# Expert order computed before the first gather, 18 weight places from the start, overflow branch moved to the 29th expert, last four experts' rows added from SBUF

## The chip, the cores and the metric

One NeuronCore of a Trainium2 chip. The metric is device time in microseconds (us); the slowest core is the only one.

## What is computed

512 tokens of width 1024 go through two blocks in fp32. The first has a Fourier branch, latent attention and a squared-relu MLP; the second a convolution and mLSTM mixer and then the mixture of experts that the change is about. Cut to that part:

```python
grp = argmax(h @ rg_w + rg_b)                 # 4 groups of 8 experts
top_val, top_idx = lax.top_k(expert_logits[grp], 2)
gate = p_grp * softmax(top_val)
for e in range(32):                           # rows routed to e
    y = (silu(xs @ w_gate[e]) * (xs @ w_up[e])) @ w_down[e]   # 1024 -> 512 -> 1024
    out[rows of e] += gate * y
return rmsnorm(x + out, final_norm_g)
```

Each expert has 6 MB of weights, so 192 MB are read, whatever the routing.

## The kernel before

The first 1097 us (both blocks up to the router) hold nothing that the change touches. There the Stream object has already queued the first expert weights.

**Weights.** A piece is 1 MB (128 x 2048 fp32); an expert has two each of gate, up and down, 192 in all, loaded in the order in which PE uses them: gate and up of expert 0, gate and up of expert 1, down of expert 0, gate and up of expert 2, down of expert 1, and so on. `Stream.issue` (L386 is its transfer) issues them all on SP's queue, and each waits until the load six places ahead of it has landed, or two places ahead in the last 24 loads. `Stream.slot` assigns places in a fixed cycle of 18: seven tiles of pool "we", three of pool "w", eight tiles "wm", of which the last two ("wo") are opened only behind the branch described below; until then `fill` (L1889) lets 16 loads go. A place is reused after PE has read its last half.

**Order of the experts.** Places 0 to 2 of the sequence are fixed experts (FIX = 3). The other 29 are taken by the number of rows that they received, so that tile shapes fit: "wide" places with up to 128 rows (L2003 and L2048), "few" with 64 (L1976, L2039), "quad" with 32 (L1990, L2032). The generator `by_count` (L1908) ranks the experts in four pieces that `gate_up(0)` runs between its own matmuls; its tile `order` is written by L1928, SP reads a register from it for each expert (L398 in `nth`) and uses it as an address. `slots` (L1760, matmuls L1765) and `slot_cols` (L1781) compute row numbers and gate weights for every place.

**Rows.** POOL gathers an expert's rows from DRAM (`gather`, L1816), PE transposes them (`xpose`, L1843), `gate_up` and `hidden_T` (L2019) compute silu(g) * u turned round, `down` the product, and POOL scatters the result to `y` in DRAM (L2053).

**Branch.** After `gate_up(0)` all engines read `last` and take tc.If (L2066) if some expert got more rows than its place holds; its body handles the surplus with small loads on SP (L2082). With these inputs the body is skipped. In program order it stands between the slot matmuls and `xpose(1)` on PE, and among the first dynamic loads on SP.

**End.** For four blocks of 128 tokens, X (the residual x3d) and two halves of y are loaded (`final_loads`, L2157 and L2159) before the last four experts (LASTS = 4) are done, added, normalised and stored (`final_rows`, L2174). The rows of the last four experts then come separately: after their scatters POOL gathers those rows again (L2149), DVE adds and scales them (L2215 to L2221), and POOL scatters them over the output (L2222); the program's close is L2242.

Of the kernel before, what the change touches and what calls it, by code (L numbers as in the profile page):

```python
# [256 lines left out]
def mixer_kernel(ctx: ExitStack, tc: tile.TileContext, io, out, stop=None, dbg=None):  # L257
# [80 lines left out]
    class Stream:  # L338
# [3 lines left out]
        def __init__(self):  # L342
# [4 lines left out]
            self.keep = []  # L347
# [13 lines left out]
        def slot(self, i):  # L361
            j = i - self.first
            if i < 10 and i not in self.ub.values():
                return self.start.tile([128, 2048], F32, tag="w0", name="w0", bufs=7)
            r = j % 18
            if j < 0 or 6 < r < 10:
                return ws.tile([128, 2048], F32, tag="w", name="w", bufs=self.WB)
            return self.keep[r if r < 7 else r - 3]

        def issue(self, upto, queue=nc.sync):  # L370
# [3 lines left out]
            while self.issued[x] <= min(upto, (self.first, len(self.items))[x] - 1):  # L374
# [12 lines left out]
                if x:  # L387
                    n = 6 if len(self.items) - i > 24 else 2
# [1222 lines left out]
    st.keep += [WE.tile([128, 2048], F32, name=f"we{i}") for i in range(7)]  # L1611
# [72 lines left out]
    st.keep += [LE.tile([128, 2048], F32, name=f"wm{i}") for i in range(6)]  # L1684
# [104 lines left out]
    queue_slots(0, A0, pos8)  # L1789
    idxf, idyf = slots("f", RE, [A0], codef, FIX)  # L1790
    later = {}
# [89 lines left out]
    closed("rq")  # L1881
    eunits = [(n, e, h, j) for e, ns in eorder for h in range(2) for j in range(2) for n in ns]
# [4 lines left out]
    passed = [0]  # L1887

    def fill():  # L1889
# [18 lines left out]
    def by_count():  # L1908

        k4 = scratch[0:32, 288:416].rearrange("p (a b) -> p a b", a=4)  # L1910
        kc = scratch[0:32, 488:490]
        rk = scratch[:, 416:424]
        ohr = scratch[:, 0:256].rearrange("p (a b) -> p a b", a=8)
        id32 = ident[0:32, 0:32]
        dve.tensor_tensor(k4[:, 0], key[0:32], id32, op=OP.mult)
        dve.tensor_reduce(kc[:, 0:1], k4[:, 0], AX.X, OP.add)
        dve.tensor_scalar(k4[:, 1], key[0:32], kc[:, 0:1], None, op0=OP.is_gt)
        dve.tensor_reduce(kc[:, 1:2], k4[:, 1], AX.X, OP.add)
        dve.tensor_scalar(k4[:, 2], id32, kc[:, 1:2], None, op0=OP.mult)
        dve.tensor_scalar(k4[:, 3], cst[0:32, 3, 0:32], kc[:, 1:2], None, op0=OP.is_equal)  # L1920
        yield 1
        prk = pmm(128, 64)
        pe.matmul(prk[:, 0:32], ones[0:32], k4[:, 2], start=True, stop=True)
        pe.matmul(prk[0:1, 32:64], pcol[0:32], k4[:, 3], start=True, stop=True)
        order = RE.tile([1, 32], I32, name="order")
        dve.tensor_copy(order, prk[0:1, 32:64])
        st.order = order
        dve.tensor_tensor(ohr, oh8, prk[:, None, 0:32].to_broadcast([128, 8, 32]), op=OP.mult)  # L1928
# [95 lines left out]
    def down(i):  # L2024
        e = seq[i]
        y, h = yt(i), hT[i]
# [28 lines left out]
        if i >= NE - LASTS:  # L2055
            wait_for(scattered[-1], none)

# [7 lines left out]
    rv = nc.values_load(last, min_val=0, max_val=S)  # L2065
    with tc.If(rv > 0):  # L2066
        OV = opened("ov", side="right")
        more = []
        fill_place(code, oh8, 32)
        fill_parts(code, oh8, 32)  # L2070
# [175 lines left out]
```

## Time and profile before

| | |
|---|---|
| runs | 1676.5, 1670.79, 1667.84 us; median 1670.79 |
| profiled execution | 1677.21 us; span 1675.3 us; mean granted TensorE clock 0.954 |
| PE busy | 1507.1 us (90%) |
| DVE, ACT, POOL busy | 713.3 us (43%), 515.2 us (31%), 143.0 us (9%) |
| traffic | 337.77 MB, mean 202 GB/s |
| chain that ended last | DMA 18%, PE 11% of the span |

The times in all rows count from the start of the span. The share of PE is an average: the first 1097 us are one stage, the experts from there to the end another, and the rows below belong to the second.

### The profile page before, as it was taken

How to read it: one execution, taken by the hardware profiler on the slowest of the kernel's cores; microseconds unless marked ns; L12 is line 12 of the kernel's file. 1: busy time of each engine (PE TensorE's matmuls, PEld its weight loads, DVE VectorE, ACT ScalarE, POOL GpSimd, SP SyncE). 2: the span in 40 equal slices, each digit the busy share in tenths (PEclk: the TensorE clock that was granted, in tenths of full speed). 3: DMA queues.
4: the chain of work that ended last, by engine and by line, in shares of the span. 5: the costliest groups of instructions: out<-in, count | busy, mean ns of one | idle time of the engine just before them, and what ended most of it. 6: DMA issues, size and time to landing. Idle time of an engine off the chain costs nothing. (4 is left out here: it accounts for less than half of the span.)

```text
span 1675.3 us, 20140 instructions
## 1 busy us (share of the span) xinstructions
PE 1507.1 (90%) x7857; PEld 1015.2 (61%) x7857; DVE 713.3 (43%) x1251; ACT 515.2 (31%) x852; POOL 143.0 (9%) x162
## 2 busy tenths in 40 slices
PE   5999999999999999999899999958999999977642
PEld 3887577788878888888657767724444444322210
DVE  5757665635663443435637967541111110100023
ACT  3454654534341323224314474300111110111101
POOL 1102310000000000000000000231110111100001
PEclk9999999999999999999999999978999999989865
DMA  9321831032222222222243223558999999999893
GB/s 369 116 84 63 322 147 51 32 121 100 84 101 101 101 77 99 101 90 87 77 117 115 97 101 116 189 186 329 378 418 419 417 403 393 404 404 413 332 371 139
DMA packets 65447, 337.77 MB, mean 202 GB/s; under 512 B 10884, under 2 KB 20268, under 8 KB 28356
## 3 DMA queue, kind: packets, MB, share of 16 engines
q1 hardware_dynamic: 54656, 318.27, 49.4%
q0 software_dynamic: 7328, 11.60, 2.1%
q10 hardware_dynamic: 3364, 6.58, 1.4%
q8 instruction: 63, 1.03, 0.2%
q14 instruction: 36, 0.29, 0.1%
HBM read 328.28 MB, written 16.78 MB: 206 GB/s over the span
## 5 line engine op out<-in xcount | busy, mean ns | idle before, releaser
L418 ACT CAST wh<-w 128x1024 fp32r<-128x1024 f32 (+1 forms) x140 | 145.5, 1041 | 366.1 <-PE mm L495 306.2
L420 DVE TENSOR_TENSOR wl<-w,wh 128x1024 fp32r<-128x1024 f32 x136 | 165.8, 1220 | 164.5 <-ACT wh L418 156.7
L496 PE MATMUL mm<-h2H,wl 128*128 128x512 f32 x256 | 101.4, 397 | 0.5 <-DVE wl L420 0.5
L495 PE MATMUL mm<-h2L,wh 128*128 128x512 f32 x256 | 101.6, 397 | 0.0
L494 PE MATMUL mm<-uH,wh 128*128 128x512 f32 x256 | 101.5, 396 | 0.0
L496 PE MATMUL mm<-uH,wl 128*128 128x512 f32 x256 | 101.3, 397 | 0.0
L495 PE MATMUL mm<-uL,wh 128*128 128x512 f32 x256 | 101.3, 396 | 0.0
L494 PE MATMUL mm<-h2H,wh 128*128 128x512 f32 x256 | 100.4, 398 | 0.0
L2003 PE MATMUL mm<-we,xgT 128*128 128x512 f32 x160 | 74.2, 612 | 0.0
L2003 PE MATMUL mm<-wm,xgT 128*128 128x512 f32 x160 | 70.2, 593 | 0.0
L1273 DVE SCALAR_TENSOR_TENSOR xT<-mm,mod,xT 128x512 f32<-128x512 f32 x32 | 24.0, 751 | 99.9 <-PE mm L496 99.9
L495 PE MATMUL mm<-hL,wh 128*128 128x512 f32 x152 | 61.5, 405 | 2.7 <-DVE hL L499 2.7
L494 PE MATMUL mm<-hH,wh 128*128 128x512 f32 x152 | 62.8, 413 | 0.3 <-ACT hH L772 0.3
L496 PE MATMUL mm<-hH,wl 128*128 128x512 f32 x152 | 61.3, 403 | 0.0
L496 PEld LDWEIGHTS mm<-h2H,wl 128*128 128x128 f32 x256 | 48.2, 188 | 12.6 <-DVE wl L420 1.0
L494 PEld LDWEIGHTS mm<-h2H,wh 128*128 128x128 f32 x256 | 48.2, 188 | 11.9 <-ACT wh L418 0.4
L495 PEld LDWEIGHTS mm<-uL,wh 128*128 128x128 f32 x256 | 48.2, 188 | 11.8
L494 PEld LDWEIGHTS mm<-uH,wh 128*128 128x128 f32 x256 | 48.2, 188 | 11.8
L496 PEld LDWEIGHTS mm<-uH,wl 128*128 128x128 f32 x256 | 48.2, 188 | 11.7
L495 PEld LDWEIGHTS mm<-h2L,wh 128*128 128x128 f32 x256 | 48.2, 188 | 11.6
L2003 PEld LDWEIGHTS mm<-we,xgT 128*128 128x128 f32 x160 | 30.8, 197 | 36.2 <-issue 36.0
L2003 PEld LDWEIGHTS mm<-wm,xgT 128*128 128x128 f32 x160 | 30.0, 190 | 36.0 <-issue 35.4
(626 smaller groups left out, 3079.3 us busy)
## 6 DMA issues: line engine op xcount, KB each, us to landing
w<-in_wd_dram SPq DMA_DIRECT2D x72, 1024.0 KB, 4.8
we<-in_eg_dram SPq DMA_DIRECT2D x34, 1024.0 KB, 15.4
wm<-in_eg_dram SPq DMA_DIRECT2D x30, 1024.0 KB, 15.7
wm<-in_eu_dram SPq DMA_DIRECT2D x30, 1024.0 KB, 15.0
we<-in_eu_dram SPq DMA_DIRECT2D x23, 1024.0 KB, 15.2
w<-in_ed_dram SPq DMA_DIRECT2D x22, 1024.0 KB, 16.2
wm<-in_ed_dram SPq DMA_DIRECT2D x22, 1024.0 KB, 15.4
we<-in_ed_dram SPq DMA_DIRECT2D x20, 1024.0 KB, 15.3
```

What stands on the lines that cost most here:

```text
L418: act.copy(h[:, :n], w)
L420: eng.tensor_tensor(l[:, :n], w, h[:, :n].bitcast(F32), op=OP.subtract)
L494: pe.matmul(o, lh, rh, start=start, stop=False)
L495: pe.matmul(o, lh, rl, start=False, stop=False)
L496: pe.matmul(o, ll, rh, start=False, stop=stop)
L1273: dve.scalar_tensor_tensor(xT[:, m], p, mod[:, 0, 40 + m:41 + m], xT[:, m], op0=OP.mult, op1=OP.add)
L2003: pe.matmul(p, x[k], w[:, z * 512:z * 512 + 512], start=k == 0, stop=k == KC - 1)
```

## The change

1. The ranking that gives `order` (and `places`, a copy for the later steps) is moved from `by_count` to a place ahead of `slots("f", ...)`, before the first gather.
2. The two last places ("wo") are opened before `gate_up(0)`. Places come from a free list instead of a fixed cycle; `fill` issues while a place is free, less `kept[0]` of them.
3. A load waits for the load three ahead of it in the first 18 and in the last 24 loads, and six ahead elsewhere.
4. The branch becomes `beyond_rows`, called at the 29th place (i = N0 = 28); its body loads on ACT's queue instead of SP's.
5. The quad buffer `yq` has two copies instead of three. For the last four places POOL clears the row tile before gathering.
6. The last four experts' rows are copied from PSUM into one SBUF tile `yl`, 32 rows each, not scattered. `final_loads` loads all four blocks at i = 29. At the end PE loads X of three blocks into PSUM by products with `ident`, adds `yl` by products with one-hot matrices `pick`, and all four blocks are squared, scaled and stored there. The last four scatters, POOL's gathers of those rows and the scatter over the output are gone.

```diff
-            r = j % 18
-            if j < 0 or 6 < r < 10:
+            if j < 0:
                 return ws.tile([128, 2048], F32, tag="w", name="w", bufs=self.WB)
-            return self.keep[r if r < 7 else r - 3]
+            self.place[j] = self.free.pop(0)
+            return self.take(self.place[j])
+
+        def take(self, p):
+            return ws.tile([128, 2048], F32, tag="w", name="w", bufs=self.WB) if p == "w" else p
...
-                    n = 6 if len(self.items) - i > 24 else 2
+                    n = 6 if i - self.first > 17 and len(self.items) - i > 24 else 3
...
+    places = scratch[:, 492:524]
+    k4 = scratch[0:32, 288:416].rearrange("p (a b) -> p a b", a=4)
+    kc = scratch[0:32, 488:490]
+    id32 = ident[0:32, 0:32]
+    dve.tensor_tensor(k4[:, 0], key[0:32], id32, op=OP.mult)
+    dve.tensor_reduce(kc[:, 0:1], k4[:, 0], AX.X, OP.add)
+    dve.tensor_scalar(k4[:, 1], key[0:32], kc[:, 0:1], None, op0=OP.is_gt)
+    dve.tensor_reduce(kc[:, 1:2], k4[:, 1], AX.X, OP.add)
+    dve.tensor_scalar(k4[:, 2], id32, kc[:, 1:2], None, op0=OP.mult)
+    dve.tensor_scalar(k4[:, 3], cst[0:32, 3, 0:32], kc[:, 1:2], None, op0=OP.is_equal)
     idxf, idyf = slots("f", RE, [A0], codef, FIX)
+    prk = pmm(128, 64)
+    pe.matmul(prk[0:1, 32:64], pcol[0:32], k4[:, 3], start=True, stop=True)
+    pe.matmul(prk[:, 0:32], ones[0:32], k4[:, 2], start=True, stop=True)
+    order = RE.tile([1, 32], I32, name="order")
+    dve.tensor_copy(order, prk[0:1, 32:64])
+    act.copy(places, prk[:, 0:32])
...
-            ys[i] = LE.tile([128, 256], F32, name="yq", tag="yq", bufs=3) if quad(seq[i]) else h3[2 + wide.index(i) % 2]
+            ys[i] = LE.tile([128, 256], F32, name="yq", tag="yq", bufs=2) if quad(seq[i]) else h3[2 + wide.index(i) % 2]
...
+    WO = opened("wo", side="right")
+    st.free += [WO.tile([128, 2048], F32, name=f"wm{i}") for i in range(6, 8)]
+    
+    st.order = order
...
+            st.free.append(st.place[passed[0]])
             passed[0] += 1
-        q = st.issued[1] - st.first
-        while q < len(last_of) and (q < 16 or len(st.keep) == 15 and q < 18 + passed[0]):
-            st.issue(st.first + q)
-            if st.issued[1] - st.first == q:
-                return
-            q += 1
+        while st.issued[1] < len(st.items) and len(st.free) > kept[0]:
+            st.issue(st.issued[1])
...
+            if i >= NE - LASTS:
+                n = 32 * (i - NE + LASTS)
+                for q in range(4):
+                    (dve.tensor_copy if q % 2 else act.copy)(yl[n:n + 32, q * 256:q * 256 + 256], p[32 * q:32 * q + 32, 0:256])
+                return
...
+    def beyond_rows():
+        rv = nc.values_load(last, min_val=0, max_val=S)
+        with tc.If(rv > 0):
...
+                    act.dma_start(t, src[bass.ds(e, 1)].rearrange("o p n -> (o p) n")[:, j * 512:j * 512 + 512])
+                    return t
...
+    def final_loads():
+        for i in range(4):
+            X.append(st.take(st.free.pop(0)))
+            Y.append(st.take(st.free.pop(0)))
             r = slice(i * 128, i * 128 + 128)
             nc.sync.dma_start(X[i][:, 0:D], x3d[r])
             for z, o in enumerate((X[i][:, D:], Y[i][:, 0:D])):
                 ld = nc.sync.dma_start(o, y2[z * S + i * 128:z * S + i * 128 + 128])
-                for f in scattered[:N0] + [none]:
+                for f in scattered + [none]:
...
+        if i == N0:
+            beyond_rows()
+            yl = h3[0]
+            pick = h3[1][:, 0:512].rearrange("p (i t) -> p i t", i=4)
+            for n in range(4):
+                dve.tensor_scalar(pick[:, n], cst[:, 3], lt[:, 0:1], -128.0 * n, op0=OP.subtract, op1=OP.is_equal)
...
+            if gathered >= N0:
+                pool.memset(xg(gathered), 0.0)
...
+        if i == N0 - 2:
+            kept[0] = 8
+        if i == N0 + 1:
+            assert len(st.free) >= 8
+            kept[0] = 0
+            final_loads()
+        if i > N0 + 1:
+            sums_of_rows(2 * (i - N0 - 2))
         if i == NE - 1:
-            final_rows(0)
+            P = [pbig() for _ in range(2)]
+            P = [[p[:, n] for n in halves] for p in P] + [[pmm() for _ in halves]]
+            for m in range(3):
+                for z, n in enumerate(halves):
+                    pe.matmul(P[m][z], ident, X[m][:, n], start=True, stop=False)
     down(NE - 1)
...
+    P.append([pmm() for _ in halves])
+    for m in range(4):
+        for z, n in enumerate(halves):
+            pe.matmul(P[m][z], pick[:, m], yl[:, n], start=m == 3, stop=True)
+    x3 = X[3][:, 0:D]
+    for z, n in enumerate(halves):
+        dve.tensor_tensor(x3[:, n], x3[:, n], P[3][z], op=OP.add)
+    ss = WO.tile([128, 4, 2], F32, name="ss")
+    for m in range(4):
+        o = Y[m][:, D:]
+        for z, n in enumerate(halves):
+            act.activation(o[:, n], P[m][z] if m < 3 else x3[:, n], AF.Square, accum_out=ss[:, m, z:z + 1])
+        if m % 2:
+            a = slice(m - 1, m + 1)
+            dve.tensor_tensor(fs[:, a], ss[:, a, 0], ss[:, a, 1], op=OP.add)
+            dve.tensor_scalar(v[:, a], fs[:, a], 1.0 / D, EPS, op0=OP.mult, op1=OP.add)
+            r = rsqrt(WO, v[:, a], 2)
+            for k in range(m - 1, m + 1):
+                o = Y[k][:, D:]
+                for z, n in enumerate(halves):
+                    dve.scalar_tensor_tensor(o[:, n], P[k][z] if k < 3 else x3[:, n], r[:, k - m + 1:k - m + 2], fB[:, n],
+                                             op0=OP.mult, op1=OP.mult)
+                nc.sync.dma_start(out[0, k * 128:k * 128 + 128, :], o)
```

**SP behind the 16th load.** L386 (L390 in the changed kernel) is `Stream.issue`, L398 (L402) the register read. Before:

```order
L386 DMA wm_8395<-in_ed_dram 128x2048
L398 TENSOR_LOAD order
L398 ISA x2
...
L386 DMA we_8092<-in_ed_dram 128x2048
L398 TENSOR_LOAD order
L398 ISA x2
L386 DMA we_8093<-in_ed_dram 128x2048
...
L2066 COMPARE_AND_BRANCH
```

Now:

```order
L390 DMA wm_8395<-in_ed_dram 128x2048
...
L402 TENSOR_LOAD order
L402 ISA x2
L390 ISA
L390 DMA wm_8544<-in_eg_dram 128x2048
...
L390 DMA wm_8545<-in_eu_dram 128x2048
...
L390 DMA we_8090<-in_eg_dram 128x2048
L390 ISA
L390 DMA we_8091<-in_eu_dram 128x2048
L2077 TENSOR_LOAD last
L2077 ISA x2
L390 DMA we_8092<-in_ed_dram 128x2048
```

Loads into the two later places follow the first register reads, and the branch no longer stands among the first dynamic loads.

**PE at the end of expert 0.** L1843 (L1864) is the transpose of the next expert's rows, L2019 (L2026) `hidden_T`, L2003 (L2010) the gate and up matmuls. Before:

```order
L1781 MATMUL mm<-code,A_8532 128x6x14
L2065 TENSOR_LOAD last
L2066 COMPARE_AND_BRANCH
...
L2066 UNCONDITIONAL_BRANCH
L1843 MATMUL big<-cst,h_8108 128x128 x8
L2019 MATMUL mm<-cst,es 128x128 x4
L1843 MATMUL big<-cst,h_8107 128x128 x8
L2003 MATMUL mm<-we_8094,xgT 128x512
```

Now:

```order
L1956 MATMUL mm<-cst,pm 1x128
L2010 MATMUL mm<-we_8092,xgT 128x512
L2010 MATMUL mm<-we_8093,xgT 128x512
...
L1864 MATMUL big<-cst,h_8108 128x128 x4
L1785 LDWEIGHTS A
L1785 MATMUL mm<-code,A 128x6x18
...
L1864 MATMUL big<-cst,h_8107 128x128 x8
L2026 MATMUL mm<-cst,es 128x128 x4
L2010 MATMUL mm<-we_8094,xgT 128x512
```

The slot matmuls stand earlier, and PE goes from the transposes to the second expert with no branch between.

**SP at the end.** L2157, L2159 (L2163, L2165) are the loads of X and y, L2174 (L2245) the output stores. Before:

```order
L2159 DMA we_8091<-y 128x1024
L386 ISA
L386 DMA w<-in_ed_dram 128x2048
...
L386 DMA wm_8390<-in_ed_dram 128x2048
L386 ISA
L386 DMA wm_8391<-in_ed_dram 128x2048
L2174 DMA out_dram<-wm_9255 128x1024
L2174 DMA out_dram<-we_8091 128x1024
```

Now:

```order
L390 DMA we_8090<-in_eg_dram 128x2048
L2078 COMPARE_AND_BRANCH
...
L2078 UNCONDITIONAL_BRANCH
L390 ISA
L390 DMA we_8091<-in_eu_dram 128x2048
...
L390 DMA wm_8395<-in_eu_dram 128x2048
L2165 DMA we_8096<-y 128x1024
...
L390 DMA wm_8544<-in_ed_dram 128x2048
...
L2245 DMA out_dram<-w 128x1024 x2
L2245 DMA out_dram<-wm_8391 128x1024
```

The branch stands eleven weight loads before the last; all loads of y come ahead of the last four weight loads; all four stores come at the very end.

## Rows read from the trace of the kernel before

**Rows 1.** Busy time by window: us, PE, PEld, DVE, ACT, POOL (count), PEclk, DMA share, GB/s.

```profile
1112.00:1130.00 18.00, 17.28 (x50) 8.68 (x51) 4.37 (x13) 1.28 (x1) 5.44 (x9) 0.83 0.01 1
...
1170.00:1187.00 17.00, 17.00 (x45) 7.70 (x43) 0.75 (x1) 1.23 (x3) 1.04 (x1) 1.00 0.79 293
1187.00:1330.00 143.00, 143.00 (x861) 68.99 (x859) 16.86 (x32) 19.05 (x33) 20.32 (x20) 0.99 1.01 416
```

**Rows 2.** Waits of SP's queue, 1097 to 1145: total us, times, longest us.

```profile
SPq L398 <- DVE rstd L1928: 27.6, 1, 27.6
SPq L2066 <- SPq L2066: 5.8, 1, 5.8
```

**Rows 3.** Timeline of SP, 1097 to 1146: start us, us, what.

```profile
1130.29 1.33 SPq L386 DMA_DIRECT2D we<-in_ed_dram  x2
1140.87 0.35 SPq L386 DMA_DIRECT2D wm<-in_eg_dram  x1
```

**Rows 4.** Timeline of PE around the branch, with the wait in brackets.

```profile
1131.46 0.84 PE L1781 MATMUL mm<-code,A 128*128 128x108 bf16 x16
1139.69 1.94 PE L1843 MATMUL big<-cst,h 128*128 128x128 f32 x8 [7.38 <-PEq L2066]
...
1143.98 2.23 PE L2003 MATMUL mm<-we,xgT 128*128 128x512 f32 x3
```

**Rows 5.** Chain that ended last, 1290 to 1360.

```profile
1302.17 6.87 PE mm L2003 x16
...
1330.31 16.24 DMA wm<-in_eu_dram
```

**Rows 6.** Busy time by window, second part of the experts.

```profile
1330.00:1548.00 218.00, 193.88 (x1013) 80.08 (x1011) 22.89 (x40) 27.48 (x48) 27.60 (x28) 0.98 1.01 405
1548.00:1558.50 10.50, 8.61 (x40) 2.85 (x40) 1.17 (x2) 2.80 (x5) 0.90 (x1) 1.00 0.57 210
1558.50:1583.50 25.00, 15.89 (x128) 5.96 (x132) 1.19 (x3) 3.16 (x6) 1.79 (x2) 0.77 0.96 361
1583.50:1600.00 16.50, 9.60 (x88) 3.97 (x80) 0.77 (x2) 1.58 (x4) 1.00 (x1) 0.72 1.00 384
...
1558.50:1650.50 92.00, 47.97 (x393) 18.32 (x393) 20.82 (x39) 11.55 (x24) 5.20 (x5) 0.70 0.95 363
```

**Rows 7.** Timeline of SP at the last 24 loads.

```profile
1543.31 0.33 SPq L386 DMA_DIRECT2D we<-in_eu_dram  x1
1556.09 0.33 SPq L386 DMA_DIRECT2D we<-in_eg_dram  x1
```

**Rows 8.** Timeline of all engines after the last weights.

```profile
1650.50 1.93 PE L2032 MATMUL mm<-wm,hT 128*32 128x256 f32 x16 [0.47 <-DMA wm<-in_ed_dram]
...
1652.50 0.37 ACT L2033 COPY yq<-mm 128x256 f32<-128x256 f32 x1 [7.65 <-PE mm L2032]
...
1664.78 0.16 DVE L515 SCALAR_TENSOR_TENSOR nwt<-nwt 128x1 f32<-128x1 f32 x1
...
1666.54 1.02 POOL L2222 DMA_INDIRECT out_dram<-h,li  x1 [8.16 <-DVE h L2221]
```

**Rows 9.** Timelines of ACT, DVE and PE elsewhere.

```profile
1130.29 0.69 ACT L2004 ACTIVATE es<-mm,scf 128x512 f32<-128x512 f32 x1 [13.46 <-PE mm L2003]
...
1131.58 0.75 DVE L2005 SCALAR_TENSOR_TENSOR es<-mm,scf,es 128x512 f32<-128x512 f32 x1 [4.58 <-PE mm L1765]
...
1506.06 1.07 PE L2032 MATMUL mm<-we,hT 128*32 128x256 f32 x16
```

**Rows 10.** DMA issues: count, KB each, us to landing.

```profile
h3d<-h SPq DMA_DIRECT2D x8, 256.0 KB, 2.6
...
out_dram<-wm SPq DMA_DIRECT2D x3, 512.0 KB, 6.8
...
out_dram<-h,li POOLq DMA_INDIRECT x1, 2.6
```

**Rows 11.** Waits of SP's queue after 1650.

```profile
SPq L2242 <- PEq L2242: 5.3, 2, 4.8
```

More of the change, by code (lines that the diff above doesn't have):

```diff
@@ L346, in __init__ @@
             self.issued = [0, 0]
-            self.keep = []
+            self.free = []
+            self.place = {}
             self.taken = 0
@@ L1610, in mixer_kernel @@
     WE = opened("we", side="right")
-    st.keep += [WE.tile([128, 2048], F32, name=f"we{i}") for i in range(7)]
+    st.free += [WE.tile([128, 2048], F32, name=f"we{i}") for i in range(7)] + 3 * ["w"]
     st.issue(st.first + 6)
@@ L1683, in mixer_kernel @@
     LE = opened("le")
-    st.keep += [LE.tile([128, 2048], F32, name=f"wm{i}") for i in range(6)]
+    st.free += [LE.tile([128, 2048], F32, name=f"wm{i}") for i in range(6)]
     with tc.issue_after(x3w[-1].ins):
@@ L1908, in by_count @@
     def by_count():
-        k4 = scratch[0:32, 288:416].rearrange("p (a b) -> p a b", a=4)
-        kc = scratch[0:32, 488:490]
         rk = scratch[:, 416:424]
         ohr = scratch[:, 0:256].rearrange("p (a b) -> p a b", a=8)
[L1914 to L1928, printed above, removed]
+        dve.tensor_tensor(ohr, oh8, places[:, None].to_broadcast([128, 8, 32]), op=OP.mult)
         dve.tensor_reduce(rk, ohr, AX.X, OP.add)
@@ L2025, in down @@
         e = seq[i]
-        y, h = yt(i), hT[i]
+        h = hT[i]
+        if i < NE - LASTS:
+            y = yt(i)
         if quad(e):
@@ L2123, in mixer_kernel, with last_rows @@
     fB = RE.tile([128, D], F32, name="fB")
     N0 = NE - LASTS
-    stores = []
+    assert quad(seq[N0]) and not quad(seq[N0 - 1]) and yt(N0 - 1) is h3[3]
     fs = WO.tile([128, 4], F32, name="fs")
     v = WO.tile([128, 4], F32, name="fv")
+    lt = WO.tile([128, 4], F32, name="lt")
     X, Y = [], []
-    def last_idx():
-        f = RE.tile([128, 4], F32, name="lf")
-        ids = RE.tile([128, 3], I32, name="li")
+    def last_rows():
+        ids = WO.tile([128, 1], I32, name="li")
         for n in range(LASTS):
@@ L2136, in last_idx @@
             e = seq[N0 + n]
[L2137 to L2155 removed]
+            dve.tensor_copy(lt[r, 1:2], later["y"][r, e:e + 1])
+        dve.tensor_tensor(lt[:, 1:2], lt[:, 1:2], cst[:, 4, 112:113], op=OP.subtract)
+        dve.tensor_scalar(lt[:, 1:2], lt[:, 1:2], 0.25, None, op0=OP.mult)
+        dve.tensor_scalar(lt[:, 2:3], lt[:, 1:2], S - 0.5, -float(S), op0=OP.is_ge, op1=OP.mult)
+        dve.tensor_tensor(lt[:, 0:1], lt[:, 1:2], lt[:, 2:3], op=OP.add)
+        dve.tensor_copy(ids, lt[:, 1:2])
+        return ids
+    def final_loads():
+        for i in range(4):
+            X.append(st.take(st.free.pop(0)))
+            Y.append(st.take(st.free.pop(0)))
             r = slice(i * 128, i * 128 + 128)
@@ L2196, in mixer_kernel @@
             p = pbig()
-            for z in range(2):
-                pe.matmul(p[:, z * 512:z * 512 + 512], ident[0:2, z:z + 1].to_broadcast([2, 128]), frow, start=True, stop=True)
+            for z, n in enumerate(halves):
+                pe.matmul(p[:, n], ident[0:2, z:z + 1].to_broadcast([2, 128]), frow, start=True, stop=True)
             act.copy(fB, p)
-        if i >= NE - 3 and i < NE - 1:
-            a = 2 * (i - NE + 3)
-            assert last_of[len(last_of) - 18 + 2 * a + 3] < nu[0]
-            final_loads(a)
@@ L2219, in mixer_kernel @@
-    dve.tensor_scalar(gs[:, 1:2], gs[:, 0:1], 1.0 / D, EPS, op0=OP.mult, op1=OP.add)
-    r = rsqrt(WO, gs[:, 1:2], 1)
-    dve.scalar_tensor_tensor(lz, lx, r, fB, op0=OP.mult, op1=OP.mult)
-    sc = pool.indirect_dma_start(out=out[0], out_offset=bass.IndirectOffsetOnAxis(ap=ids[:, 0:1], axis=0), in_=lz, in_offset=None,
-                                 bounds_check=S - 1, oob_is_err=False)
-    for f in stores:
-        wait_for(sc, f)
+        if i == N0 - 2:
[4 more added lines that the diff above has]
+            final_loads()
@@ new lines, in mixer_kernel @@
+    x3 = X[3][:, 0:D]
[13 more added lines that the diff above has]
+                o = Y[k][:, D:]
+                for z, n in enumerate(halves):
+                    dve.scalar_tensor_tensor(o[:, n], P[k][z] if k < 3 else x3[:, n], r[:, k - m + 1:k - m + 2], fB[:, n],
+                                             op0=OP.mult, op1=OP.mult)
+                nc.sync.dma_start(out[0, k * 128:k * 128 + 128, :], o)
```

148 lines of the change are left out of this document (56 added, 92 removed).

## The prediction

> **What bounds the kernel now.** I read the counts of busy time by window first, then the waits of SP's queue, the timelines around the two places where traffic stops, the chain of waits, and last the tail. The two kernels issue the same work until the router is done, so everything below lies behind 1097 us of the span.
>
> The expert stage moves 192 weight pieces of 1 MB through SP's queue into 16, later 18, places in SBUF. [rows 1] shows its phases, and the DMA column matters most. From 1112 to 1130 almost nothing moves (1 GB/s): all 16 places are full, and SP waits for the order of the experts, 27.6 us of it [rows 2]. The loads restart at 1130.29, are cut again by the branch, and go on at 1140.87 [rows 3]. PE has its own hole: its last matmul before the branch starts at 1131.46, the next at 1139.69 after 7.38 us behind the branch, and the second expert's gate and up begin at 1143.98 [rows 4]. Then, the decisive row: from 1170 to 1187 the DMA share is 0.79 at 293 GB/s while PE is busy for 17.00 of 17 us. The loads had filled every place and waited for PE to free them. So by 1187 the 18 us of silence had been made up, and what the loads could fetch was set by the moment at which PE freed places. From 1187 to 1330 both are full (PE 143.00 of 143 us, 416 GB/s); the stock of full places is eaten, and at 1330.31 the chain changes from PE's matmuls to loads [rows 5]. From there to the end the loads are the bound.
>
> [rows 6] has this second part: 405 GB/s until 1548 with six loads in flight, a hole of 210 GB/s where the rule changes from six to two, then 363 GB/s on average over the last 92 us. PE is busy for 47.97 us of those 92. After the last weights, the tail from 1650.50 to the end of the span at 1675.3 takes 24.8 us and is a serial chain [rows 8].
>
> **The change part by part.** All sums are made against the profiled execution, 1677.2 us; it stands 6.4 us above the median of the runs shown (1670.79), and I subtract the same difference from the median.
>
> *A. Start.* The branch leaves the place after expert 0's gate and up, the slot matmuls move between the halves of that gate and up, and the transposes follow directly. The hole of 7.38 us goes; what remains is the handover. Second expert's matmuls: 1143.98 before, about 1137 now. I take **-7.2** (between -4, if half of the hole returns as a wait for the slots or for expert 0's silu, and -8.5, if the handover before L1843 vanishes too). As PE's frees set the loads' stock at 1187, and the loads set the end, the whole later stage moves with this. The earlier order and the two early places cost and gain nothing more: 29 register reads (32 experts less the three fixed ones) at about 0.57 us (27.6 us of waiting end near 1124.5, ten reads later the first load is issued at 1130.29 [rows 2, 3]) lie in the 18 us of silence; if the order came no earlier than before, the loads would start at 1130 as now, and the slack of the 0.79 row, 17 x 0.21 = 3.6 us, covers half of the shift only. Three in flight for the first 18 loads cost nothing: these land before 1112 and the first of the dynamic ones are not needed until after 1137.
>
> *B. The switch.* In before SP issues nothing between 1543.31 and 1556.09 [rows 7], and the window of 10.5 us runs at 210 instead of 405 GB/s: 10.5 x (1 - 210/405) = 5.1 us lost. Going from six to three instead of two leaves two loads, not one, in flight at the emptiest point. I take half, **-2.5** (0 to -5.1).
>
> *C. The last 24 loads.* Before: 92 us at 363 GB/s are 33.4 MB. The four output stores (2.1 MB) leave this stretch for the tail: 31.3 MB. With two weight loads in flight the row is 361 GB/s; where two weights and half-MB loads overlapped, about three in flight, it is 384; with six it is 405 [rows 6]. The first 17 loads, 17.8 MB, at 384 take 46.4 us; the other 13.5 MB, where half-MB loads come on top, at 405 take 33.3 us; 79.7 together. The branch now stands on SP between load 180 and 181, and its untaken side waits until all of SP's transfers have landed. That empties the pipe of three loads once. Nearest row: the switch's 5.1 us [rows 6]; nothing below, and above the time of three whole loads, 3 x 1.05 MB / 384 = 8.2 us. I take 4.5. Together 84.2 instead of 92: **-7.8** (from 92 to 31.3/0.405 = 77.3 us, -14.7; to 31.3/0.361 + 8.2 = 94.9 us, +2.9). PE and ACT also meet the branch here; the hole of 7.38 us is covered by PE's 44 idle us in this stretch. The y loads that SP issues between load 187 and the last four wait for expert 27's scatter; its weights are loads 170 and 171, at 1.05/0.384 = 2.7 us each some 40 us earlier: nothing. If that cover were gone, the four loads behind on SP would slip with it. Two yq buffers for three and POOL's memsets of gathered rows: nothing, since POOL is busy for 5.20 of the 92 us.
>
> *D. The tail.* Before: 24.8 us from the last down product at 1650.50. Now the rows stay in SBUF: no scatter, no gathers, no scattered store, but the adding is done by PE and all four blocks are finished at the end. Last down product 1.9 [rows 8]; four copies that ACT and DVE make in turn, 0.37 each plus handover, 1.9; eight one-hot products, which are 16 PE instructions of 512 columns: 6.87 at full clock [rows 5]. PE's granted clock in the last 92 us is 0.70 and it has idled just before, as in 1650.50, where 16 instructions took 1.93 against 1.07 at full clock [rows 8, 9]; at 0.65, 10.6. Behind the last product two additions on DVE and the last two squares on ACT, 0.75 x 2 + 0.69 x 2 [rows 9] = 2.9. Then DVE: 16 small operations at 0.2 (the series that ends at 1664.78 is eight steps of 0.19 [rows 8]) and eight scalings at 0.75, 9.2, because in its order the first pair's scaling stands behind the second pair's sum. Store: 0.33 to issue, and between 2.6 us (256 KB) and 6.8 us (512 KB under load) to land [rows 10], I take 3.9. The end: before, the last scatter is issued at 1666.54, lands 2.6 us later, and of the 6.2 us to the end 4.8 are SP's wait for the other engines' close [rows 8, 11], behind POOL's transfer; without it 1.4. The sum is 1.9 + 1.9 + 10.6 + 2.9 + 9.2 + 4.2 + 1.4 = 32.1, **+7.3** (from -2.5, with full clock, a 2.6 us landing and the first pair's work hidden; to +13.9, at half clock, 13.7 us, and 6.8 us to land).
>
> Sum: -7.2 - 2.5 - 7.8 + 7.3 = **-10.2**: 1667.0 for a run like the profiled one, **1661** for the median.
>
> **Rivals.** *R1: the third load in flight gives nothing.* If two in flight already take what the queues give, the last stretch keeps 363 GB/s: 31.3/0.363 + 4.5 = 90.7, C is -1.3, B is 0, and the sum -1.2: **1670**. For it: the row of two in flight shows a share of 0.96 [rows 6], nearly full. Against it: the GB/s beside that share are 361, not 405, so full shares are not full traffic. The Trainium skill, "DMA: Bandwidth & Descriptors", section "Anatomy of one DMA — SWDGE (gpsimd) path", gives a transfer a fixed part of about 2.0 us and its bytes at 436 GB/s; by that fit 1 MB takes 4.4 us and two in flight would offer 477 GB/s, so that an estimate from the page finds two sufficient, and with it R1. The trace disagrees: 361 measured with two.
>
> *R2: slower, the branch in the full stage.* Where the branch stood, queues were nearly idle; now each engine jumps while 384 GB/s run. If SP's jump waits behind the queued loads and the pipe then refills from nothing, one round of three loads costs 8.2 us; three rounds, 24.6 instead of my 4.5, give **1681**. It decides from some 23 us of standstill on. For it: SP waited 5.8 us [rows 2] and PE 7.38 us [rows 4] there even with little traffic. Against it: those holes are well below 23 us, and SP's untaken side holds no loads of the body any more, so its jump is short. The Trainium skill, "Runtime: NRT & Kernel Launch", section "Instruction fetch mechanics", says that a taken branch whose target lies outside the pages already fetched costs a DMA fetch of the target page. PE's 7.38 us agree.
>
> *R3: the silence is regained in full.* If bytes alone bound the end, 18 us of standstill count instead of 7.2: -18 - 2.5 - 7.8 + 7.3 = -21, **1650**. Against it: the 0.79 row, where loads wait for places.
>
> *R4: the start does not move.* If PE at the second expert waits for the slots or the transposed rows until about 1144, A is 0 and the sum -3.0: **1668**. For it: in before silu and slots end only at about 1132 [rows 9].
>
> **Numbers.** About 0.5%, 8.4 us, is what a measurement of this kernel can tell from no change: faster means below 1662.4. My forecast has 0.54 (own range 1654 to 1667): 0.40 below that line, 0.14 within. R1 0.22: 0.03 faster, 0.16 same, 0.03 slower, if its tail is at the long end. R2 0.08, slower. R3 0.12, faster. R4 0.04, same. Together faster 0.55, same 0.34, slower 0.11. The range 1645 to 1673 takes in R3, R1 and R4 and the bounds of the tail, and leaves out R2 and the far ends of A, C and D.
>
> **What would show it.** A: PE's first matmul of the second expert at about 1137 and no wait on a branch there. B and C: over 375 GB/s in the stretch from the switch to the branch, a hole of some 5 us on SP once, and the last weights landing about 17 us earlier than 1650.50 (1633). D: a tail of 32 us after them, with PE's one-hot products 9 to 12 us and no POOL transfer. I am wrong if the loads stay near 361 GB/s (R1), if the hole at the branch is over 20 us (R2), if the last weights land before 1625 (R3), or if the tail is over 39 us.

## The result, and the profile after

The changed kernel takes **1649.8 us** (median of 4 runs, 1646.2 to 1653.2) against 1672.2 us: ratio 0.9866, 95% interval 0.9831 to 0.9901. The forecast was 1661 with a range of 1645 to 1673; the direction holds, the gain is twice what I gave. It lies below the forecast's own range (1654 to 1667); the wide range holds it because that also took in the 1650 of rival R3 and the lower bound of the tail.

The profiled execution takes 1646.16 us (span 1644.3), 31.0 us less than the profiled one of before. Not all of that is the change: the first gate-and-up matmul of expert 0, behind a thousand microseconds of the same work, starts at 1114.71 in the one and at 1109.96 in the other. In the runs of this case it starts anywhere from 1109.96 to 1118.52. So I measure from that matmul, and give totals by medians. Timeline of PE, before (the first line is expert 0's own transposes):

```profile
1112.72 1.94 PE L1843 MATMUL mm<-cst,h 128*128 128x128 f32 x8 [10.48 <-DMA h<-h3d,idxf]
...
1114.71 8.86 PE L2003 MATMUL mm<-we,xgT 128*128 128x512 f32 x16
```

and after:

```profile
1107.97 1.94 PE L1864 MATMUL mm<-cst,h 128*128 128x128 f32 x8 [8.48 <-DMA h<-h3d,idxf]
...
1109.96 8.13 PE L2010 MATMUL mm<-we,xgT 128*128 128x512 f32 x16
...
1118.44 7.03 PE L2010 MATMUL mm<-we,xgT 128*128 128x512 f32 x16
1125.31 0.60 PE L1864 MATMUL big<-cst,h 128*128 128x128 f32 x4
1125.74 0.84 PE L1785 MATMUL mm<-code,A 128*128 128x108 bf16 x16
1126.42 1.50 PE L1864 MATMUL big<-cst,h 128*128 128x128 f32 x12
1127.76 0.60 PE L2026 MATMUL mm<-cst,es 128*128 128x128 f32 x4
```

These answer to [rows 4]: no wait on a branch, and the second expert's matmuls begin at 1128.20. From expert 0 to the next it is 18.24 us, where it was 29.27.

The windows after (us, PE, PEld, DVE, ACT, POOL with counts, PEclk, DMA share, GB/s) answer to [rows 1, 6]:

```profile
1112.00:1130.00 18.00, 18.00 (x89) 9.69 (x88) 5.76 (x24) 2.98 (x3) 6.05 (x6) 1.00 0.57 207
1130.00:1145.00 15.00, 15.00 (x37) 6.63 (x36) 0.75 (x1) 0.69 (x1) 0.00 (x0) 1.00 0.82 305
1145.00:1170.00 25.00, 25.00 (x64) 11.34 (x63) 2.04 (x3) 1.65 (x3) 2.05 (x2) 1.00 0.85 314
1170.00:1187.00 17.00, 17.00 (x173) 8.98 (x175) 3.14 (x7) 2.92 (x7) 3.35 (x4) 1.00 1.00 388
...
1526.00:1537.00 11.00, 9.15 (x38) 2.94 (x38) 0.48 (x2) 1.35 (x3) 0.00 (x0) 1.00 0.80 333
1537.00:1568.60 31.60, 11.55 (x95) 4.42 (x94) 1.09 (x2) 4.61 (x9) 2.69 (x3) 0.80 0.99 385
1568.60:1576.00 7.40, 1.35 (x14) 0.77 (x18) 1.55 (x6) 0.00 (x0) 0.00 (x0) 0.50 0.76 316
1576.00:1622.40 46.40, 31.90 (x322) 13.98 (x314) 14.72 (x21) 5.07 (x13) 0.00 (x0) 0.81 0.95 385
...
1537.00:1622.40 85.40, 44.80 (x423) 19.17 (x422) 17.37 (x29) 9.68 (x22) 2.69 (x3) 0.78 0.95 379
...
1622.40:1631.60 9.20, 8.21 (x32) 3.38 (x32) 1.54 (x3) 4.09 (x13) 0.00 (x0) 1.00 0.01 2
```

Four things stand there. PE has no idle time from 1112 to 1187, at granted clock 1.00 where the first of these windows had 0.83 [rows 1]. The queues are still not full until 1170, now because the loads wait for places; the wait table of SP from 1110 to 1300 names the main releaser (31.2 of its 31.5 us lie before 1170):

```profile
SPq L390 <- PE mm L2010: 31.5, 10, 8.4
```

From the switch on it is 385 GB/s with three in flight on both sides of the branch, 379 with the branch in it. The drain at the branch is 7.4 us at 316 GB/s, between two loads 7.65 us apart; SP's waits in 1560 to 1600 (total, times, longest):

```profile
SPq L2078 <- SPq L2078: 6.6, 4, 2.5
```

The tail, from the chain of waits that ended last (start, us, what), answers to [rows 8]:

```profile
1622.46 1.11 PE mm L2041 x16
...
1624.46 1.98 PE big L2226 x4
1626.45 1.73 PE mm L2226 x4
...
1629.65 2.31 ACT w L2234 x8
1631.96 0.58 ACT wm L2234 x2
...
1634.52 2.64 DVE w L2243 x4
...
1639.06 1.32 DVE wm L2243 x2
```

It lasts from 1622.46 to 1644.3, 21.8 us, against 24.8. The split of the change, by distances in the two traces: start -11.0 (18.24 for 29.27), from there to the first of the last 24 loads -3.3 (408.8 for 412.1), from that load to the last down product -8.9 (85.5 for 94.4), tail -3.0. Together -26.2; the medians say -22.4. There is one trace of the kernel before, from its slowest execution (1677.21 us; the others took 1667.84 to 1676.5), so some us of the parts can be chance.

### The profile page after: what moved, and what is told of

The parts are those of the page before. It is cut to its first block, busy times and chain, and to the rows that moved or that the text cites. A ratio compares the mean times of both kernels' runs of the same rounds, so it can differ in the third digit from the quotient of the medians.

```text
span 1644.3 us, 20192 instructions
## 1 busy us (share of the span) xinstructions
PE 1497.1 (91%) x7885; PEld 1011.1 (61%) x7885; DVE 713.6 (43%) x1258; ACT 516.6 (31%) x863; POOL 135.4 (8%) x158
## 3 DMA queue, kind: packets, MB, share of 16 engines
q8 instruction: 65, 1.06, 0.3%
## 5 line engine op out<-in xcount | busy, mean ns | idle before, releaser
L2010 PE MATMUL mm<-we,xgT 128*128 128x512 f32 x160 | 72.5, 601 | 0.0
L2010 PE MATMUL mm<-wm,xgT 128*128 128x512 f32 x160 | 71.9, 605 | 0.0
L2010 PEld LDWEIGHTS mm<-wm,xgT 128*128 128x128 f32 x160 | 30.5, 194 | 36.6 <-issue 36.0
L2010 PEld LDWEIGHTS mm<-we,xgT 128*128 128x128 f32 x160 | 30.3, 193 | 35.6 <-issue 34.8
## 6 DMA issues: line engine op xcount, KB each, us to landing
wm<-in_eg_dram SPq DMA_DIRECT2D x31, 1024.0 KB, 15.4
wm<-in_eu_dram SPq DMA_DIRECT2D x31, 1024.0 KB, 15.2
wm<-in_ed_dram SPq DMA_DIRECT2D x22, 1024.0 KB, 15.2
we<-in_ed_dram SPq DMA_DIRECT2D x22, 1024.0 KB, 15.2
```

The costliest lines, as they stand in the source:

```text
L2010: pe.matmul(p, x[k], w[:, z * 512:z * 512 + 512], start=k == 0, stop=k == KC - 1)
```

## The experiments

All medians, ratios (to the kernel before, in the same session) and distances. D1 runs from expert 0's first gate-and-up matmul to the next expert's, D2 to the last down product, D3 to the end of the span. The kernel before had medians of 1670.7 to 1673.8 us beside these runs, so across sessions the ratios compare better than the us.

| kernel | us | ratio, 95% interval | D1 | D2 | D3 |
|---|---|---|---|---|---|
| before | 1672.2 | | 29.3 | 535.8 | 560.6 |
| changed | 1649.8 | 0.9866 (0.9831 to 0.9901) | 18.2 | 512.5 | 534.3 |
| e1 two in flight | 1659.3 | 0.9919 (0.9900 to 0.9938) | 19.1 | 522.5 | 547.2 |
| e2 no branch | 1646.6 | 0.9844 (0.9825 to 0.9863) | 18.6 | 510.3 | 532.1 |
| e3 branch early | 1658.8 | 0.9910 (0.9888 to 0.9932) | 26.3 | 522.3 | 544.2 |
| e4 order late | 1649.8 | 0.9866 (0.9844 to 0.9888) | 18.0 | 513.2 | 535.0 |
| e5 no ident products | 1652.7 | 0.9868 (0.9846 to 0.9890) | 19.1 | 514.8 | 537.1 |
| e6 old ending, no branch | 1654.2 | 0.9881 (0.9866 to 0.9896) | 18.8 | 513.7 | 538.3 |
| e7 four in flight | 1648.8 | 0.9857 (0.9837 to 0.9876) | 18.5 | 513.4 | 535.2 |
| e8 six in flight | 1651.0 | 0.9857 (0.9837 to 0.9877) | 18.2 | 513.5 | 535.3 |
| e9 two places late | 1652.8 | 0.9883 (0.9863 to 0.9904) | 16.8 | | 533.8 |
| e10 six, three at the branch | 1650.2 | 0.9867 (0.9844 to 0.9889) | 18.9 | 514.3 | 536.2 |
| e11 six, no branch | 1649.1 | 0.9864 (0.9844 to 0.9884) | 18.2 | | 532.2 |
| e12 six, body's loads on POOL | 1649.5 | 0.9864 (0.9838 to 0.9891) | 18.9 | 509.6 | 531.5 |

(In e4 and e9 PE does half of the next expert's transposes before expert 0's first gate-and-up matmul, so their distances start about 1.7 us later; counted from expert 0's own transposes, D3 is 536.3 in the changed kernel, 538.8 in e4 and 537.6 in e9. In e9 and e11 the last down products run in one group, and D2 isn't comparable. D1 is 18.2 to 19.1 in the ten traces whose start is that of the changed kernel, so a few tenths of a us in it say nothing.)

**e1, two loads in flight in the last 24.**

```diff
-  n = 6 if i - self.first > 17 and len(self.items) - i > 24 else 3
+  n = 2 if len(self.items) - i <= 24 else 6 if i - self.first > 17 else 3
```

> The changed kernel with two loads in flight instead of three in the last 24 loads. Theory (the third load was worth about 9 us: in the trace the stretch from the first of these loads to the last weights took 94.4 us before and 85.5 after): that stretch comes back to 92 to 95 us, and the time is 1657 to 1660 us. Rival (two loads already take what the queues give, and the gain came from the stores leaving the stretch): the stretch stays at 85 to 87 us and the time within 2 us of 1650.

9.5 us slower than the changed kernel. Its windows around the switch and behind it, then the second one in three parts, before, in and behind the drain at the branch:

```profile
1530.00:1543.40 13.40, 10.93 (x50) 3.75 (x50) 1.42 (x3) 2.42 (x4) 0.90 (x1) 1.00 0.71 295
1543.40:1634.20 90.80, 51.97 (x414) 20.19 (x410) 16.57 (x27) 8.58 (x20) 1.80 (x2) 0.76 0.91 352
...
1543.40:1564.90 21.50, 11.31 (x86) 4.07 (x82) 0.00 (x0) 3.53 (x7) 1.80 (x2) 0.84 0.94 328
1564.90:1571.80 6.90, 2.78 (x26) 1.47 (x30) 1.55 (x6) 0.00 (x0) 0.00 (x0) 0.59 0.64 256
1571.80:1634.20 62.40, 37.89 (x306) 14.65 (x298) 15.02 (x21) 5.05 (x13) 0.00 (x0) 0.74 0.94 370
```

Over the whole stretch 352 GB/s where three give 379, and 328 against 385 between switch and branch. The stretch takes 90.9 us, less than the 92 expected, 5.4 more than with three; the way from the second expert to the first of the last 24 loads grows by 3.8 us (412.6 for 408.8), the tail by 2.8. The third load is worth its time: R1 falls. With two in flight the branch also comes five weight loads earlier, and the loads of y stand ahead of the last ten weight loads instead of the last four; what that adds is not separated.

By the Trainium skill, "DMA: Bandwidth & Descriptors", section "Anatomy of one DMA — SWDGE (gpsimd) path", the estimate worked out from its fit for two transfers of 1 MB in flight was 477 GB/s. That fit is for transfers issued by GpSimd. Here SP issues them, and this run shows 328 to 370 outside the drain.

**e2, no branch; e3, the branch behind expert 0 again.** Of the changed kernel, e2 drops the call, and e3 moves it ahead of the loop over the experts:

```diff
         if i == N0:
-            beyond_rows()
```
```diff
     gathered = 2
+    beyond_rows()
```

> The changed kernel without the overflow branch (its body is skipped with these inputs). Theory (the emptied pipe at the 29th place costs a few us once): the hole between two loads on SP of 7.65 us goes, the last weights land 3 to 5 us earlier, 1645 to 1647 us. Rival 1 (the drain is made up by later loads): 1650. Rival 2 (the branch in the full stage costs more than its hole shows, since PE stood still for 19.6 us): 1640 or less.

> The changed kernel with the branch back behind expert 0's gate and up, all else as changed. Theory (PE's hole at the start sets the whole stage, because the loads wait for places that PE frees): from the first gate-and-up matmul of expert 0 to that of the next expert 25 to 28 us instead of 18.2, the drain near the end goes, and the time is 1649.8 + 8 - 4 = 1653 to 1657 us. Rival (bytes alone bound the end, the first loads are out already, and the PE hole is hidden): 1645 to 1647 us, as without the branch.

By medians the branch costs 3.2 us at the 29th place (1649.8 - 1646.6; the runs overlap, and by D2 and D3 it is 2.2) and 12.2 at the first (1658.8 - 1646.6; the runs lie apart, and by D2 and D3 it is 12.0). Timeline of PE in e3:

```profile
1131.68 0.84 PE L1785 MATMUL mm<-code,A 128*128 128x108 bf16 x16
1138.01 1.08 PE L1864 MATMUL big<-cst,h 128*128 128x128 f32 x4 [5.49 <-PEq L2078]
1139.97 1.12 PE L1864 MATMUL big<-cst,h 128*128 128x128 f32 x4 [0.88 <-SPq L2078]
1140.88 1.06 PE L2026 MATMUL mm<-cst,es 128*128 128x128 f32 x4
```

The hole is 6.4 us (5.49 + 0.88), and what follows it runs at the lower clock level: the four transposes take 1.08, not 0.60, `hidden_T` 1.06, not 0.60. That is how 6.4 us of waiting become 7.6; the other 0.4 of the 8.0 in D1 lies in expert 0's first sixteen products. The next eighteen products still take 9.91 us instead of 7.95. SP is through its branch at about 1140, yet issues its next load at 1150.42, 8.2 us behind the second expert's first matmul: it waits for PE to free a place. The rival of e3, a hidden hole, is out: D2 grows by 9.8.

The Trainium skill, "Runtime: NRT & Kernel Launch", section "Instruction fetch mechanics", says that a taken branch whose target lies outside the pages already fetched waits for a DMA fetch of the target page. The 5.49 us on PE's sequencer would fit, but no run separates a fetch from the rest of that wait.

**e4, the ranking back inside expert 0; e9, the two places given later.**

```diff
     def by_count():
+        dve.tensor_tensor(k4[:, 0], key[0:32], id32, op=OP.mult)
...
+        dve.tensor_copy(order, prk[0:1, 32:64])
+        st.order = order
```
```diff
-    st.free += [WO.tile([128, 2048], F32, name=f"wm{i}") for i in range(6, 8)]
+    wo = [WO.tile([128, 2048], F32, name=f"wm{i}") for i in range(6, 8)]
...
+        if i == 1:
+            st.free += wo
```

> The changed kernel with the ranking of the experts back inside expert 0's gate and up, so that the order is known about 20 us later; branch, places and tail as changed. Theory (loads that start late catch up, because they wait for places until about 1170): SP waits some 20 us for the order, the first expert-to-expert distance stays 18 to 20 us, and the time is 1649 to 1653 us. Rival (the silent 18 us of the queues count in full): the loads restart some 10 us later and the time is 1658 to 1662 us.

> The changed kernel with the two extra places given to the loads only after expert 0's gate and up. Theory (loads wait for places that PE frees until about 1170 us, so two places earlier are no gain by themselves): 1649 to 1651 us. Rival (the two extra places are stock that lasts to the end, 2 MB or 5 us of loading): 1653 to 1656 us.

By medians e4 ends where the changed kernel ends, 1649.8. Its windows:

```profile
1112.00:1130.00 18.00, 18.00 (x61) 9.40 (x60) 4.13 (x13) 3.17 (x4) 5.63 (x9) 0.90 0.34 123
1130.00:1145.00 15.00, 14.84 (x72) 7.64 (x71) 5.24 (x24) 0.69 (x1) 6.09 (x6) 1.00 1.00 408
1145.00:1170.00 25.00, 25.00 (x65) 11.27 (x64) 2.79 (x4) 1.65 (x3) 2.05 (x2) 1.00 0.87 331
```

84 GB/s fewer in the first 18 us, 103 more in the next 15, then the same wait for places. Counted from expert 0's own transposes its trace is 2.4 us longer, 1.5 of them before the second expert; its rival asked for 8 to 12. R3 falls: making the queues silent again cost nothing by medians, and at most those 2.4 us. For e9 the median is 3 us above, within its runs' spread (1647.0 to 1653.7), and its trace is 1.2 us longer by the same count: no gain of 5 us from the two places is seen, but a smaller one isn't excluded.

**e5, no ident products.** The residual of three blocks is left out of the sums.

```diff
-            for m in range(3):
-                for z, n in enumerate(halves):
-                    pe.matmul(P[m][z], ident, X[m][:, n], start=True, stop=False)
...
-            pe.matmul(P[m][z], pick[:, m], yl[:, n], start=m == 3, stop=True)
+            pe.matmul(P[m][z], pick[:, m], yl[:, n], start=True, stop=True)
```

> The changed kernel without the twelve products of X with ident that PE makes while the last weights load; the residual of three blocks is left out of the sums, the one-hot products and all that follows stay. Theory (these products keep PE's granted clock at its upper level, and that is why the one-hot products took 7.15 us and not the 10.6 of the forecast): PE idles before the last down products, the first one-hot products run at the lower level (3.8 us for four instead of 2.0), the sixteen take 9 to 13 us, and the tail grows from 21.8 us by 2 to 6: 1652 to 1656 us. Rival (the down products alone keep the clock up): sixteen in 7.2 us, 1649 to 1651 us.

```profile
1626.44 1.93 PE L2041 MATMUL mm<-we,hT 128*32 128x256 f32 x16 [0.65 <-DMA we<-in_ed_dram]
1628.83 1.51 PE L2041 MATMUL mm<-we,hT 128*32 128x256 f32 x16 [0.45 <-DMA we<-in_ed_dram]
1631.28 1.98 PE L2223 MATMUL big<-h,h 128*128 128x512 f32 x4 [0.94 <-DVE h L2045]
```

My theory fell: without the ident products the down products run at the lower level (1.93), but the last of them is already faster (1.51), and the first four one-hot products take 1.98 us as in the changed kernel; all sixteen 7.1. In e1, where PE had waited 2.89 us just before the last down product, the same four took 3.78:

```profile
1634.28 1.89 PE L2041 MATMUL mm<-we,hT 128*32 128x256 f32 x16 [2.89 <-DMA we<-in_ed_dram]
1637.08 3.78 PE L2226 MATMUL big<-h,h 128*128 128x512 f32 x4 [0.91 <-DVE h L2045]
1640.65 2.16 PE L2226 MATMUL mm<-h,h 128*128 128x512 f32 x4
```

In these two runs the level followed what PE had done just before, not the ident products as such. The total, 1652.7 us, doesn't separate the theories (runs 1647.6 to 1656.0; the ratio is that of the changed kernel).

**e6, the ending of before, without the branch** (it has no branch either, so it is compared with e2).

```diff
-            if i >= NE - LASTS:
...
-                return
+        if i >= NE - LASTS:
+            wait_for(scattered[-1], none)
...
+    final_rows(2)
+    for c, o in ((1, ly), (2, lz)):
+        g = rows_of(y2, c, o, 2 * S)
```

> The changed kernel without the branch, as in e2, but with the ending of the kernel before: the last four experts' rows are scattered, gathered again and scattered over the output, and the output stores of all four blocks go out beside the last loads. Compared with e2 (1646.6 us, tail 21.85 us after the last weights). Theory (the new ending is shorter by what the trace shows, 24.8 against 21.8 us, and keeps the stores out of the load stretch): the last weights land 1 to 3 us later, the tail is 24 to 26 us, 1650 to 1653 us. Rival (as forecast, the old ending is the shorter one by 7 us, paid with up to 5 us of stores in the load stretch): 1640 to 1645 us.

7.6 us slower than e2 by medians of two sessions; against the kernel before in each session the ratios are 0.0037 apart, 6.2 us, and by D3 it is 6.2 too. So the new ending is the better one by about 6 us, the upper end of the theory, and far from the forecast's price. Its last pieces:

```profile
1627.55 1.93 PE L2040 MATMUL mm<-we,hT 128*32 128x256 f32 x16 [2.99 <-DMA we<-in_ed_dram]
...
1633.12 1.04 POOL L2160 DMA_INDIRECT h<-y,li  x1 [1.89 <-DMA y<-yq,idy]
...
1643.55 1.03 POOL L2237 DMA_INDIRECT out_dram<-h,li  x1 [8.06 <-DVE h L2236]
```

The tail is 24.7 us (span 1652.2) against 21.9 in e2, and the last weights land 3.4 us later by D2, with two of the output stores queued ahead of the last load.

**e7, e8, e10: more loads in flight.** n = 4 in the last 24; six to the end; six to the end but three for the three loads ahead of the branch.

> The changed kernel with four loads in flight in the last 24 loads. Theory (each further load in flight raises the rate from 385 GB/s towards the 404 of six in flight, and the switch from six costs less): the stretch of 85.4 us shortens by 2 to 5 us, 1645 to 1648 us. Rival (three are enough, or a fourth delays the load that PE waits for): 1649 to 1652 us.

> The changed kernel with six loads in flight to the end. Theory of the rate alone: no switch and 404 GB/s, 31.5 MB take 78 instead of 85.4 us and the switch's loss of about 2.5 us goes: 1640 to 1643 us. Rival (with six in flight the branch drains six loads at once and the last pieces all land together, so PE's work on them is left for the end): the drain costs 2 to 3 us more and the tail 2 to 4 us: 1646 to 1651 us.

> The changed kernel with six loads in flight to the end, except for the three loads ahead of the branch, which wait for the third before them. Theory (six in flight bring 414 GB/s where three bring 370 to 385, and what ate this in the run with six was the drain at the branch, 15.2 us at 245 GB/s): the drain falls to 7 to 10 us, and the time is 1644 to 1648 us. Rival (the last weights land no earlier, as PE and the later loads set them): 1649 to 1652 us.

None is told from the changed kernel. (The order of SP's work shifts a little with the number in flight: the branch stands 11 weight loads before the end in the changed kernel, 8 in these three, 16 in e1.) The windows of e8 show why the rate did not help:

```profile
1531.00:1575.80 44.80, 24.07 (x143) 8.59 (x138) 1.59 (x3) 5.95 (x11) 3.14 (x4) 0.85 1.01 414
1575.80:1591.00 15.20, 1.72 (x18) 0.92 (x22) 1.55 (x6) 0.00 (x0) 0.00 (x0) 0.50 0.59 245
1591.00:1629.90 38.90, 30.11 (x319) 13.99 (x311) 14.76 (x21) 5.05 (x13) 0.00 (x0) 0.84 0.94 378
```

414 GB/s with six in flight, where 404 had been expected; but the drain doubles, 15.2 us at 245 GB/s (three in flight: 7.4 at 316; four: 10.1 at 263). Against 414 that is 15.2 x (1 - 245/414) = 6.2 us lost. And behind the branch six in flight give 378 GB/s, no more than three (385). So the higher rate works for 44.8 us only: it saves some 4.5 us there (44.8 us at 414 against 11.0 at 333 and 33.8 at 385), and the longer drain costs 6.2 - 1.3 = 4.9 more. In e10 the step down to three is itself a window of 10.3 us at 327, ahead of a drain of 7.7 at 266.

**e11, six in flight and no branch; e12, six in flight, and the branch's small loads on POOL**, so that SP's untaken side has no transfers to wait for.

```diff
-                    act.dma_start(t, src[bass.ds(e, 1)].rearrange("o p n -> (o p) n")[:, j * 512:j * 512 + 512])
+                    pool.dma_start(t, src[bass.ds(e, 1)].rearrange("o p n -> (o p) n")[:, j * 512:j * 512 + 512])
```

> Six loads in flight to the end and no branch (skipped with these inputs). Theory (the drain ate the rate that six in flight give): 92.5 us at 385 GB/s become 87 at 410, and the time is 1640 to 1643 us, 3 to 6 below the run with three in flight and no branch (1646.6). Rival (three in flight are as good as six): 1645 to 1648 us.

> The changed kernel with six loads in flight to the end, and with the small loads of the branch's body issued by POOL instead of ACT, so that SP's untaken side has no transfers to wait for and crosses the branch with its loads in flight; the loads of y stay ahead of the last six weight loads. Theory (with six in flight the rate is 414 GB/s, and in the run with six the 15.2 us drain at the branch ate it): no hole on SP over 5 us at the branch, the last weights land 5 to 10 us earlier, 1640 to 1645 us, less than both kernels. Rival (a later wait takes its place: the loads of y wait for the last scatter and hold the weight loads behind them): the last weights land no earlier and the time is 1647 to 1651 us.

In e11 the loads run at full rate to 1611.7 and the time is still 1649.1:

```profile
1533.00:1611.70 78.70, 48.40 (x422) 18.50 (x419) 7.23 (x18) 11.02 (x24) 2.69 (x3) 0.86 1.01 415
1611.70:1622.80 11.10, 8.54 (x12) 3.11 (x12) 9.46 (x8) 0.00 (x0) 0.00 (x0) 0.61 0.46 182
```

The y loads are now the last to land, not the weights: on SP they stand behind all weight loads (the first is issued at 1596.61), and the additions of the blocks on DVE, which were covered by weight loads, lie bare for 11.1 us. SP waits for the last scatter for 0.5 us only; why the order of its loads came out so is not shown. In e12 the drain is gone, but the last 39 us have a lower mean rate; the line after it is their end:

```profile
1575.00:1590.00 15.00, 10.13 (x112) 4.16 (x104) 1.61 (x4) 1.64 (x5) 0.00 (x0) 0.86 1.02 419
1590.00:1629.00 39.00, 21.28 (x178) 8.54 (x177) 13.19 (x17) 3.43 (x9) 0.00 (x0) 0.74 0.86 342
...
1620.00:1629.00 9.00, 8.51 (x86) 3.53 (x78) 1.62 (x4) 1.56 (x4) 0.00 (x0) 0.80 0.43 179
```

Around the y loads it is 364 GB/s (1590 to 1600), then 387 and 422, and 179 at the end, where nothing is left to issue and the last load takes 17.3 us to land. By D3 it is the shortest, 2.9 us below the changed kernel; its runs (1643.0 to 1652.9) don't show it. No version measured is clearly faster than the changed kernel.

Taken back one at a time, three parts of the change have a price that the runs show: the third load 9.5 us (e1), the branch's place 9.0 (e3 against the changed kernel), the ending 6.2 (e6 against e2). Together that is 24.7, for 22.4 measured. The early order and the two early places show none clear of the runs' spread (e4, e9). The two `yq` buffers, POOL's clearing of row tiles and three in flight in the first 18 loads were not tried alone.

## Why the prediction was right, and where its sizes were off

**What bounds the kernel** held. Loads wait for PE's places until about 1170, then the queues are full to the end but for the switch and the branch, so a PE hole at the start counts and the silence of the queues hardly does (e3 against e4). The decisive row was the 0.79 of [rows 1]. The number was partly luck: A and D came out faster than their own ranges allowed, and 1649.8 is the figure of R3, whose mechanism e4 refutes.

**A, start: -7.2 forecast, -11.0 measured**, outside the term's range (-4 to -8.5), and -10.2 to -11.1 by the ten traces with this start. I priced the hole and nothing else. 7.4 us are the hole; transposes and `hidden_T` take 2.9 us (1125.31 to 1128.20, slot matmuls in them) instead of 4.3, and expert 0's stretch before the hole is 15.4 us (1109.96 to 1125.31) instead of 17.6 (1114.71 to 1131.46 + 0.84). 0.60 for four transposes now and 1.94 for eight in [rows 4] are the two clock levels. Of the 2.2 us of expert 0's stretch 1.3 are slot and ranking matmuls that now stand elsewhere, and 0.8 lie in its first sixteen products, which vary by as much among the ten traces (8.08 to 9.00 us for all sixteen). e3 puts the branch back and gives 8.0 of the 11.0.

**B, the switch: -2.5, measured -3.3** (the distance from the second expert's first matmul to the first of the last 24 loads). The window of 11.0 us at 333 GB/s against 404 loses 1.9 us, where before 5.1 were lost. With two in flight again (e1) the distance is 412.6 us, as before; with six to the end (e8) it is 402.5.

**C, the last loads: -7.8, measured -8.9** (85.5 us for the last 24 loads, 84.2 in the sum; the sum's 92 for the kernel before starts one load later than the 94.4 here). Two misses partly offset each other. Without the branch (e2) the loads take 82.3 us where the sum has 79.7: I took 384 GB/s for three in flight, and it is 385, but also behind the branch, where I took 405. The drain I put at 4.5 loses 7.4 x (1 - 316/385) = 1.3 us of traffic; taking the branch out gains 3.2 by medians and in this stretch, 2.2 by D2 and D3. R2's standstill of 23 us is not there.

**D, the tail: +7.3, measured -3.0.** This term was mis-sized, by 10 us. Step by step, from 1622.46:

- Down product and copies until the first one-hot product: 2.0 us (3.8 in the sum). The product takes 1.1 at the upper clock, and PE starts after two of the four copies.
- Sixteen one-hot products: 7.1 (10.6).
- Additions and squares behind them: 1.5 (2.9). One addition and most squares run beside the products.
- Small operations and scalings on DVE: 7.2 (9.2). Sixteen small operations stand there as in the sum, but the two pairs' chains alternate, and they take 1.8 us instead of 3.2; the eight scalings take 5.4 instead of 6.0.
- Last store and end: 3.9 (5.6). The stores land in 2.6 us.

The largest single step is "PE's granted clock in the last 92 us is 0.70 ... at 0.65, 10.6", 3.5 of the 10 us, 4.3 with the down product; the rest is the end of the kernel (1.7) and work priced in series that overlaps. A mean over a stretch in which PE idles half the time says nothing of the level at which it runs a dense run of products. The window from 1622.40 to 1631.60 has 1.00. In e1, where PE had just waited, the same sixteen took 9.2 us, so the forecast's 10.6 is not far from a case that occurs. The lower bound, -2.5, was passed by 0.5; the upper bound's own terms add up to +13.3, not +13.9. e6 confirms the sign by itself: old ending against new, +6.2 us by D3, of which 2.8 lie in the tail and 3.4 in the landing of the last weights.

R1 fell in e1, R3 in e4, R4 in the first rows after. One sign of being wrong came up: "the last weights land before 1625 (R3)"; the last down product starts at 1622.46. But in this execution expert 0 began 4.75 us earlier than in the one before, and counted from there 1625 would be 1620.3, which was not reached. A sign of this kind needs a distance, not a time of the span. With D at -3.0 the sum would have been -20.5, and the forecast 1650.3.

## What to carry to other kernels

Ask at each stage which resource the other waits for: here, while loads waited for buffers, time lost on PE counted in full and silent queues cost next to nothing; once the queues were full, PE had time to spare, and the branch cost 2 to 3 us instead of 12. Transfers in flight are a means, not an end: three instead of two gave 9.5 us, six instead of three nothing. With the branch its drain grew (e8); without it the loads of y came last (e11). Do not price dense work at the mean granted clock of a stretch with idle time in it; take a row of the same kind of work, with the same wait before it.

## What I had not expected

The same program up to 1110 us starts expert 0 up to 8.6 us apart (1109.96 to 1118.52) from one profiled execution to another, about three times what the smaller edits here change. Distances inside one trace leave that spread out; but each kernel has one trace, and how far a distance varies from one execution to the next is not shown. And the drain at the branch grows with the loads in flight: 7.4 us at 316 GB/s with three, 10.1 at 263 with four, 15.2 at 245 with six, about 2.5 us for each load (with two, in e1, it is 6.9 us at 256). Why the last load of e12 takes 17.3 us to land, while the rate falls below half, stays open.
